# A hybrid attention and convolution layer on one core: dependent work moved between the steps of a slot

## The chip, the cores and the metric

The kernel runs on one NeuronCore of a Trainium2 chip. The metric is the device time of one execution in microseconds (us). The engines are TensorE (PE in the profile, its weight loads PEld), VectorE (DVE), ScalarE (ACT), GpSimd (POOL), and SyncE (SP), whose queue issues the loads. They run side by side, each in its own order, and wait for each other through semaphores.

## What is computed

One layer on 272 tokens (16 learned ones and 256 given ones) of width 4096, in fp32, batch 1, cut from the reference:

```python
h = rmsnorm(x, norm_g)
p = h @ w_in                       # 4096 -> 16384
q, k, v, g_attn, b_conv, c_conv, h_conv, z_conv = split(p)     # 2048 each
# 16 heads x 128, strictly causal stick-breaking attention
z = q k^T / sqrt(128)
after = reverse_cumsum(log_keep) - log_keep       # log_keep = log_sigmoid(-z), masked
o = where(mask, exp(log_sigmoid(z) + after), 0) @ v
o = group_rmsnorm(o * silu(g_attn), attn_norm_g, 16)
y = b_conv * short_conv(c_conv * h_conv, conv_w)  # depthwise, causal, 3 taps
y = group_rmsnorm(y * silu(z_conv), conv_norm_g, 16)
out = rmsnorm(x + concat([o, y]) @ w_out, final_norm_g)[16:]
```

## The kernel before

**Split products.** An fp32 product is made of three fp32r products, high by high, low by high and high by low. Each piece of weights (128 rows by 1024) arrives by DMA as `raw`; ScalarE casts it to the high part `wh` (line 411), VectorE subtracts to get the low part `wl` (`low`, line 407). Rings of six `wh` and six `wl` stand between these two engines and TensorE. The loop at line 1018 goes through `pieces`: at piece i it issues TensorE's work of i, ScalarE's cast of piece i+4, then the tasks that are due at i (`run_tasks`), then VectorE's low part of piece i+4 (`lows`). A task thus stands behind a cast and ahead of a low in the queues. The order is fixed by hand.

**Groups and slots.** The 32 heads and convolution channels are worked as eight groups of two units. For a group, q, the attention gate, b and z are made with tokens on partitions, two row blocks at a time, by a seven-product scheme (Strassen-like) over 15 of the 16 pairs of weight pieces; k, v, c and h are made per unit with features on partitions ("blocks": `mm`, four pieces of 24 matmuls each, 272 or 258 wide). The list interleaves both. A **slot** is one pair in the seven-product form and half a block: the pieces A, B, T, U, then two pieces p; T and U have no load, as their weights are sums that VectorE makes from A's and B's (lines 428, 431, 433, so B has four VectorE instructions: t, raw, wl, raw). Slots are numbered 0 to 14; slot 12 has no block. TensorE has 6, 3, 6, 6, 24 and 24 matmuls in the six pieces, those of A, B, T, U 512 wide. In a slot's six steps the fourth is U and the fifth the first p. The cast that ScalarE issues at U is that of the next slot's B, at the first p that of the next T, at the second p that of the next U.

**Zones.** Zone S of group g are its 15 slots, with blocks k, v, c, h of the first unit and k, v, c of the second; they end with slots 1, 3, 5, 7, 9, 11 and 14. The finished block is evicted by VectorE (kT, vt, cc) in the tasks of the next piece. Then comes zone R: the h block of the second unit in four pieces, with one plain pair (A, B, 12 matmuls each) of the next group in the middle. There the seven products of the group are evicted to `cq` (q and gate) and `cb` (b and z) by `evict`, eight VectorE operations of line 661.

**Banks.** PSUM has eight banks. In zone S seven hold products, and one, `d + D22`, is shared by the blocks and by all small outputs (po, ct, mx): `spare(i)` gives this list of one. In zone R three banks are spare, in the order of D22, D12, D21 of the group that has just ended; `bank` takes them in turn by a counter that runs through the whole kernel.

**The dependent work of a group** is done in the next group's zones R and S, by generators whose `yield k` puts what follows k pieces later: `silu`, `q_t` (q transposed on TensorE, copied back by ScalarE), `scores` (z, then tanh and ln on ScalarE), `weights` per head (Relu on ScalarE, two scans and a subtraction on VectorE, four Exp on ScalarE), `trans` (a 32x32 transpose on VectorE, then small ScalarE copies into `at`, in four blocks of four, and two more), `po` (the product with v, then VectorE's gate), `conv_t` and `conv_out` (the convolution transposed on TensorE, copied by ScalarE, gated on GpSimd), `squares` and `norm`, and `mix` (transposes on TensorE, ScalarE's scaling, and a DMA to `mixd` from ScalarE's queue). `v_block` and `h_block` plan v's transpose and copies (`vv`, four blocks and `v3`) and the three taps (`conv`: one ScalarE and two VectorE operations). Before the change, for group g in the slots c of group g+1 (`t[c]` is B of slot c):

```python
later(t[1], weights, g, 0)    # t[3] for the second head
later(t[2], trans, g, 0)      # after(t[4], 1) for the second
later(t[4], po, g, 0)         # t[6]
later(t[7], squares, g, "h")  # "c" two pieces after t[9]
later(t[8], conv_t, ...)      # conv_out two pieces later
later(t[10], norm, g)
later(t[12], mix, g, "h")     # "c" two pieces later
```

Tiles that are used by turns bound the order too: `zm`, `zs` and `u2` hold the stages of the attention and also vt, yv, silu's factor and mixing's outputs.

After group 7 follows the output projection, by the same seven-product scheme and with split pieces, and the final normalisation; `at`, the transposes and the norm of group 7 run at its beginning.

Of the kernel before, what the change touches and what calls it, by code (L numbers as in the profile page):

```python
# [15 lines left out]
P = 128  # L16
# [106 lines left out]
def kernel(ctx, tc, xt, xin, xm, par, fg, w1, w2, out):  # L123
# [15 lines left out]
    def bank(nm, i=None):  # L139

        if i is None:
            i = free[0][turn[0] % len(free[0])]
            turn[0] += 1
        return pp.tile([P, 512], F32, tag=f"b{i}", name=nm)
# [385 lines left out]
    def later(at, fn, *args):  # L530
        tasks.append((at, fn, args))
# [53 lines left out]
        V.tensor_tensor(out=kt, in0=src, in1=rstd, op=ALU.mult)  # L585
        hd[u, "k"] = kt

    def v_block(u, src, at_):
        vt = wk.tile([P, 448], F32, tag="zm", name=f"vt{u}")
        G.memset(vt[:, L:L + META], 0.0)  # L590
        V.tensor_tensor(out=vt[:, :L], in0=src, in1=rstd, op=ALU.mult)

        def vtrans():
            y = wk.tile([P, 416], F32, tag="zs", name=f"yv{u}")
            V.transpose(out=y[:, :L + META], in_=vt[:, :L + META])
            yield 1
            vv = wk.tile([P, 2 * P], F32, tag=f"vv{u % 2}", name=f"vv{u}")
            for i in range(4):
                blocks(vv, y[:, :2 * P], 2, i, (A.copy,))
                yield 1  # L600
            v3 = wk.tile([META, P], F32, tag=f"v3{u % 2}", name=f"v3{u}")
            for i in range(4):
                A.copy(out=v3[:, 32 * i:32 * i + 32], in_=y[32 * i:32 * i + META, 2 * P:2 * P + 32])
            hd[u, "v"] = (vv, v3)

        later(at_, vtrans)
# [6 lines left out]
    def h_block(u, src, at_):  # L613
        c = hd.pop((u, "c"))
        V.tensor_tensor(out=c, in0=src, in1=c, op=ALU.mult)  # L615

        def conv():
            y = wk.tile([P, SEQ], F32, tag=f"cy{u % 2}", name=f"cy{u}")
            w = [pt[:, CW0 + 3 * u + i:CW0 + 3 * u + i + 1] for i in range(3)]
            A.mul(out=y, in_=c[:, 0:SEQ], mul=w[0])  # L620
            yield 1
            V.scalar_tensor_tensor(out=y, in0=c[:, 1:SEQ + 1], scalar=w[1], in1=y, op0=ALU.mult, op1=ALU.add)
            V.scalar_tensor_tensor(out=y, in0=c[:, 2:SEQ + 2], scalar=w[2], in1=y, op0=ALU.mult, op1=ALU.add)
            cy[u] = y

        later(at_, conv)

    def plain_block(u, b, e):
        ps = psum.pop((u, b, "p"))
        if b == 0:  # L630
            k_block(u, ps[:, :L])
        elif b == 1:
            v_block(u, ps[:, :L], after(e, 1 if u < 2 else 6 if u % 2 else 13))
        elif b == 2:
            c_block(u, ps[:, META - 2:L])
        else:
            h_block(u, ps[:, META - 2:L], after(e, (12 if u else 8) if u % 2 == 0 else 8 if u < 15 else 1))


    gr = {}  # L640
# [44 lines left out]
    def squares(g, q):  # L685

        y = gr[g][q][1]
        if "ss" not in gr[g]:
            gr[g]["ss"] = wk.tile([P, 8], F32, tag="sm3", name=f"ss{g}")
        ss = gr[g]["ss"]  # L690
        j = wk.tile([P, P], F32, tag="junk", name=f"j{q}{g}")
        f = 0 if q == "h" else 4
        for t in range(2):
            for u in range(2):
                c = f + 2 * u + t
                A.activation(out=j, in_=y[:, t, u], func=AF.Square, scale=(rt if q == "h" else rt2)[:, t:t + 1],
                             accum_out=ss[:, c:c + 1])

    def norm(g):

        ss = gr[g]["ss"]
        r = rsqrt_raw(ss, P, EPS, *small(f"n{g}_"))
        V.tensor_tensor(out=ss, in0=r, in1=fac, op=ALU.mult)
        for f, q in ((0, "h"), (4, "c")):
            yield 1
            y = gr[g][q][1]
            for t in range(2):
                for u in range(2):
                    c = f + 2 * u + t
                    A.mul(out=y[:, t, u], in_=y[:, t, u], mul=ss[:, c:c + 1])  # L710
# [22 lines left out]

    def q_t(g):
        q = gr[g]["h"][0]
        o = bank(f"qT{g}")
        for u in range(2):
            for t in range(2):
                c = (2 * u + t) * P
                T.transpose(out=o[:, c:c + P], in_=q[:, t, u], identity=ident)  # L740
        yield 1
        A.copy(out=q, in_=o.rearrange("p (u t x) -> p t u x", u=2, t=2))

    def scores(g):
        q = gr[g]["h"][0]
        z, zm, l = {}, {}, {}
        for u in range(2):
            kt = hd[2 * g + u, "k"]
            z[u] = bank(f"z{g}_{u}")
            T.matmul(out=z[u][:, :144], lhsT=q[:, 0, u], rhs=kt[:, :144], start=True, stop=True)  # L750
            T.matmul(out=z[u][:, 144:ZW], lhsT=q[:, 1, u], rhs=kt, start=True, stop=True)
        yield 1
        for u in range(2):
            zm[u] = (wk.tile([P, 512], F32, tag="u2", name=f"zm{g}_{u}", bufs=2) if u else
                     wk.tile([P, 448], F32, tag="zm", name=f"zm{g}_{u}"))[:, :ZW]
            l[u] = wk.tile([P, 448], F32, tag=f"zl{u}", name=f"zl{g}_{u}")[:, :ZW]
            V.scalar_tensor_tensor(out=zm[u][:, :144], in0=z[u][:, :144], scalar=rq[:, 0:1], in1=zmask[:, P:],
                                   op0=ALU.mult, op1=ALU.add)
            V.scalar_tensor_tensor(out=zm[u][:, 144:], in0=z[u][:, 144:ZW], scalar=rq[:, 1:2], in1=zmask,
                                   op0=ALU.mult, op1=ALU.add)  # L760
            A.activation(out=l[u], in_=zm[u], func=AF.Abs)
        for u in range(2):
            A.activation(out=l[u], in_=l[u], func=AF.Tanh, scale=0.5)
        yield 1
        for u in range(2):
            A.activation(out=l[u], in_=l[u], func=AF.Ln, scale=0.5, bias=half)
            gr[g]["z", u] = zm[u], l[u]

    def weights(g, u):
        zm, l = gr[g].pop(("z", u))  # L770
        s = wk.tile([P, 416], F32, tag="zs", name=f"zs{g}_{u}")
        A.activation(out=s, in_=zm, func=AF.Relu)
        yield 1
        for c, n in ((0, 144), (144, L)):
            V.tensor_tensor_scan(out=l[:, c:c + n][:, ::-1], data0=s[:, c:c + n][:, ::-1],  # L775
                                 data1=l[:, c:c + n][:, ::-1], initial=0.0, op0=ALU.add, op1=ALU.subtract)
        V.tensor_tensor(out=s, in0=zm, in1=l, op=ALU.subtract)
        yield 1

        za = wk.tile([P, 512], F32, tag="u2", name=f"za{g}_{u}", bufs=2) if u else wk.tile([P, 448], F32, tag="zm", name=f"za{g}_{u}")  # L780
        za = za[:, :448]
# [8 lines left out]
    def trans(g, u):  # L790
        za = gr[g].pop(("za", u))
        y = wk.tile([P, 448], F32, tag=f"zl{u}", name=f"ya{g}_{u}")
        V.transpose(out=y, in_=za)
        yield 1
        for i in range(4):
            blocks(at[:, P:], y[:, :3 * P], 3, i, (A.copy,) if g < GROUPS - 1 else (A.copy, V.tensor_copy))
            if i < 3 and (g < GROUPS - 1 or i == 1):
                yield 1
        A.copy(out=at[:META, P - META:P], in_=y[96:96 + META, 400:416])
        A.copy(out=a3[:, P - META:], in_=y[96:96 + META, 432:448])  # L800

# [33 lines left out]

    def after(i, k):

        return real[min(nth[i] + k, len(real) - 1)]

    def slot(g, c):  # L840

        return pieces.index(("B", g, sevens(g)[c]))

    def plan_group(g):
        f = fin[g]
        e = ends[2 * g + 1, 3]
        end = g == GROUPS - 1
        later(after(f, 1), silu, g, "h")
        later(after(f, 2), q_t, g)
        later(after(f, 2), silu, g, "c")  # L850
        later(after(f, 4), scores, g)
        if not end:
            t = [slot(g + 1, c) for c in range(len(SJ))]
        later(after(f, 7) if end else t[1], weights, g, 0)
        later(after(f, 10) if end else t[3], weights, g, 1)
        later(after(f, 10) if end else t[2], trans, g, 0)
        if end:
            later(after(e, 5), conv_t, (2 * g, 2 * g + 1))
            later(after(e, 7), conv_out, g)
            later(after(f, 13), po, g, 0)  # L860
            later(after(f, 13), trans, g, 1)
            later(after(f, 17), po, g, 1)
            later(after(f, 17), squares, g, "c")
            later(after(f, 19), squares, g, "h")
            later(after(f, 20), norm, g)
            later(after(f, 22), mix, g, "h")
            later(after(f, 23), mix, g, "c")
            return
        later(t[4], po, g, 0)
        later(after(t[4], 1), trans, g, 1)  # L870
        later(t[6], po, g, 1)
        later(t[7], squares, g, "h")
        later(t[8], conv_t, (2 * g, 2 * g + 1))
        later(after(t[8], 2), conv_out, g)
        later(after(t[9], 2), squares, g, "c")
        later(t[10], norm, g)
        later(t[12], mix, g, "h")
        later(after(t[12], 2), mix, g, "c")


    res, fgs, acc, sqs = [], {}, [], []
# [274 lines left out]
```

## Time and profile before

| what | value |
|---|---|
| median of 3 runs (lowest to highest) | 1798.13 us (1797.33 to 1800.46) |
| the profiled execution, its own time | 1798.58 us |
| its span | 1796.9 us |
| granted TensorE clock over the span | 0.997 |
| HBM read and written | 391.70 MB, 13.11 MB |

In a line of the profile's groups stand the line of the kernel, the engine, the operation, what is written and read (buffer numbers left out) and its shape, the count, the busy time, the mean of one in ns, and the idle time of the engine just before with what ended it. A row of the view of waits has the engine and line that waited, what released it, the total in us, how often, and the longest. A timeline row has the start, the duration, engine, line, operation, tiles and shape; several alike are merged (x2). A row of the windows view has the stretch, its length, then for each engine its busy time and in brackets its instructions (PE, PEld, DVE, ACT, POOL), the granted clock, the DMA's busy share and GB/s. The chain that ended last runs for 89% of the span over TensorE and for 6% over VectorE. Group 5's dependent work lies in the slots of the next group, whose slot 1 begins at 1100.5 us.

### The profile page before, as it was taken

What the parts mean: (1) busy time and instruction counts of PE and PEld (TensorE: products, weight loads), DVE (VectorE), ACT (ScalarE), POOL (GpSimd) and SP (SyncE); (2) the same over time, 40 slices, a digit from 0 to 9 for tenths busy, and PEclk for the clock granted to TensorE, in tenths of its full rate; (3) what the DMA queues carried; (4) which work ended last, traced back from release to release, by engine and by line L of the source; (5) the groups of instructions that cost most, each with busy time, mean ns of one, the idle gap of its engine ahead of it and who ended that gap; (6) DMA issues with size and microseconds to landing.
All of it is one profiled execution on the core that took longest, in us unless ns stands there. A gap on an engine that the chain in (4) does not pass through costs nothing.

```text
span 1796.9 us, 29780 instructions
## 1 busy us (share of the span) xinstructions
PE 1773.2 (99%) x10947; PEld 1604.8 (89%) x10947; DVE 1563.3 (87%) x1899; ACT 1225.1 (68%) x2081; POOL 148.3 (8%) x180
## 2 busy tenths in 40 slices
PE   9999999999999999999999999999999999999997
PEld 7899989998999899989898989899989988888897
DVE  6866888998899889988898889889988988889896
ACT  6754776767676767676767677767776786555553
POOL 2133101010101010001010101011001110000000
PEclk9999999999999999999999999999999999999999
DMA  8967666766666667666666666666666676676565
GB/s 314 322 231 247 203 219 225 230 214 222 224 224 213 224 223 225 216 223 224 222 212 223 223 224 210 223 223 226 208 225 222 223 250 233 223 237 219 196 216 196
DMA packets 119667, 406.77 MB, mean 226 GB/s; under 512 B 13408, under 2 KB 18656, under 8 KB 119520
## 3 DMA queue, kind: packets, MB, share of 16 engines
q1 hardware_dynamic: 115488, 401.19, 66.5%
q10 hardware_dynamic: 4032, 3.67, 0.6%
q8 instruction: 86, 1.41, 0.3%
q14 instruction: 61, 0.50, 0.1%
HBM read 391.70 MB, written 13.11 MB: 225 GB/s over the span
## 4 chain that ended last, share of the span: by engine, by line
PE 89%; DVE 6%; issue 2%; ACT 2%; DMA 1%; ACTq 0%; DVEq 0%; SPq 0%
PE P L452 17%; PE P L454 16%; PE P L455 16%; PE mm L445 12%; PE mm L444 12%; PE mm L446 12%; DVE wl L407 3%; ACT wh L411 1%; DVE t L428 1%; DVE cb L661 1%; PE mo L944 0%; PE mo L943 0%; PE mo L942 0%; PE po L808 0%; DVE zl L775 0%
## 5 line engine op out<-in xcount | busy, mean ns | idle before, releaser
L407 DVE TENSOR_TENSOR wl<-raw,wh 128x1024 fp32r<-128x1024 f32 (+3 forms) x773 | 867.5, 1146 | 142.1 <-ACT wh L411 130.0
L411 ACT CAST wh<-raw 128x1024 fp32r<-128x1024 f32 (+3 forms) x773 | 718.9, 967 | 237.3 <-DVE raw L433 78.7
L444 PE MATMUL mm<-xs,wh 128*128 128x258 f32 (+1 forms) x2048 | 583.4, 285 | 0.0
L446 PE MATMUL mm<-xs,wl 128*128 128x258 f32 (+1 forms) x2048 | 581.9, 284 | 1.0 <-DVE wl L407 1.0
L445 PE MATMUL mm<-xs,wh 128*128 128x258 f32 (+1 forms) x2048 | 581.7, 284 | 0.0
L444 PEld LDWEIGHTS mm<-xs,wh 128*128 128x128 f32 x2048 | 385.5, 188 | 4.3 <-ACT mfc L727 0.2
L445 PEld LDWEIGHTS mm<-xs,wh 128*128 128x128 f32 x2048 | 385.6, 188 | 4.1
L446 PEld LDWEIGHTS mm<-xs,wl 128*128 128x128 f32 x2048 | 385.6, 188 | 1.5 <-DVE wl L407 1.4
L411 ACT CAST wh<-t 128x1024 fp32r<-128x1024 f32 (+1 forms) x125 | 130.3, 1043 | 194.7 <-DVE t L428 171.2
L452 PE MATMUL P<-wh,xs 128*128 128x512 f32 x499 | 196.5, 394 | 2.6 <-ACT wh L411 1.9
L455 PE MATMUL P<-wl,xs 128*128 128x512 f32 x499 | 194.9, 391 | 0.0
L454 PE MATMUL P<-wh,xs 128*128 128x512 f32 x499 | 194.8, 390 | 0.0
L452 PE MATMUL P<-wh,mixl 128*128 128x512 f32 (+1 forms) x412 | 155.7, 378 | 0.0
L455 PE MATMUL P<-wl,mixh 128*128 128x512 f32 (+1 forms) x412 | 155.1, 377 | 0.0
L454 PE MATMUL P<-wh,mixh 128*128 128x512 f32 (+1 forms) x412 | 155.0, 376 | 0.0
L428 DVE TENSOR_TENSOR t<-raw,raw 128x1024 f32<-128x1024 f32 (+1 forms) x125 | 153.0, 1224 | 0.0
L407 DVE TENSOR_TENSOR wl<-t,wh 128x1024 fp32r<-128x1024 f32 (+1 forms) x125 | 152.5, 1220 | 0.0
L452 PEld LDWEIGHTS P<-wh,xs 128*128 128x128 f32 x499 | 94.0, 188 | 24.5 <-DVE cc L615 3.0
L455 PEld LDWEIGHTS P<-wl,xs 128*128 128x128 f32 x499 | 94.1, 189 | 20.0
L454 PEld LDWEIGHTS P<-wh,xs 128*128 128x128 f32 x499 | 94.1, 189 | 19.4
L452 PE MATMUL P<-wh,lent 128*128 128x512 f32 x280 | 111.3, 397 | 0.0
L455 PE MATMUL P<-wl,lent 128*128 128x512 f32 x280 | 109.3, 390 | 0.0
(240 smaller groups left out, 2128.8 us busy)
## 6 DMA issues: line engine op xcount, KB each, us to landing
raw<-w SPq DMA_DIRECT2D x614, 512.0 KB, 4.3
lent<-sumd SPq DMA_DIRECT2D x70, 512.0 KB, 5.6
raw<-w SPq DMA_DIRECT2D x32, 384.0 KB, 3.9
sumd<-lent SPq DMA_DIRECT2D x10, 512.0 KB, 4.7
raw<-xin SPq DMA_DIRECT2D x8, 512.0 KB, 5.1
raw<-mixd SPq DMA_DIRECT2D x8, 512.0 KB, 4.5
xr<-xt SPq DMA_DIRECT2D x15, 272.0 KB, 5.0
res<-xin SPq DMA_DIRECT2D x12, 256.0 KB, 4.7
```

What stands on the lines that cost most here:

```text
L407: nc.vector.tensor_tensor(out=lo[:, c], in0=t[:, c], in1=h[:, c].bitcast(F32), op=ALU.subtract)
L411: nc.scalar.copy(out=h[:, c], in_=t[:, c])
L428: nc.vector.tensor_tensor(out=s[:, :2 * hw].rearrange("p (a b) -> p a b", a=2), in0=a[:, :2 * hw].rearrange("p (a b) -> p a b", a=2), in1= ...
L444: nc.tensor.matmul(out=o, lhsT=h, rhs=x[:, 0, s:], start=k == 0, stop=False)
L445: nc.tensor.matmul(out=o, lhsT=h, rhs=x[:, 1, s:], start=False, stop=False)
L446: nc.tensor.matmul(out=o, lhsT=lo, rhs=x[:, 0, s:], start=False, stop=k == KC - 1)
L452: nc.tensor.matmul(out=o, lhsT=a[1], rhs=h, start=key not in begun, stop=False)
L454: nc.tensor.matmul(out=o, lhsT=a[0], rhs=h, start=False, stop=False)
L455: nc.tensor.matmul(out=o, lhsT=a[0], rhs=lo, start=False, stop=last)
L661: V.tensor_tensor(out=o, in0=x, in1=y, op=op)
```

## The change

The dependent work is put at other pieces. `slot(g, c, q)` now gives the piece of kind q (A, B, T, U, "p" or "q" for the second p) of a slot, and a generator may `yield "U"` or `yield "p"`: what follows goes to the next U, or to the next first p of a slot (outside zone S to the next piece). In group g+1's slots the work of group g now stands so: head 0's Relu at U of 2, its scans at p of 2, its Exp at U of 3; head 1's at p of 3, p of 4, p of 5. The transposes of the weights at p of 3 and T of 6, their copies two blocks at the next U, one at the p, one and the small ones at the U after. The convolution's transposes go from slot 8 to B of 4, `conv_out` to U of 4, po to B of 6 and B of 8, squares of c to p of 7 and U of 8, those of h to U of 9, the norm to A of 10 with all its eight muls at U of 10; mixing stays at B and U of 12. v's VectorE transpose goes to p of 8 and U of 12, its copies to p of 9 and following, and, for the second unit, to U and p of slots 0 and 1 of the next group; the taps' first operation to U of 8, or U of slot 1, and VectorE's part to the p after. q takes the third spare bank of zone R (D21), the scores' two the second and the first. The last group keeps its places except for what `yield` joins and splits.

```diff
-    def v_block(u, src, at_):
+    def v_block(u, src, at_, at2):
...
-            yield 1
+            later(at2, vcopies, y)
+
+        def vcopies(y):
             vv = wk.tile([P, 2 * P], F32, tag=f"vv{u % 2}", name=f"vv{u}")
-            for i in range(4):
+            for i, k in enumerate((0, 1, 1, 1) if u < 2 else (0, 0, "p", "U") if u % 2 else (0, "p", "U", 0)):
+                if k:
+                    yield k
                 blocks(vv, y[:, :2 * P], 2, i, (A.copy,))
-                yield 1
+            yield 1 if u < 2 else "p"
...
             A.mul(out=y, in_=c[:, 0:SEQ], mul=w[0])
-            yield 1
+            yield "p"
...
-            v_block(u, ps[:, :L], after(e, 1 if u < 2 else 6 if u % 2 else 13))
+            g = u // 2
+            v_block(u, ps[:, :L], *((after(e, 1), after(e, 2)) if not g else
+                                    (slot(g, 12, "U"), slot(g + 1, 0, "U") if u < 15 else slot(g, 13, "U")) if u % 2 else
+                                    (slot(g, 8, "p"), slot(g, 9, "p"))))
...
-            h_block(u, ps[:, META - 2:L], after(e, (12 if u else 8) if u % 2 == 0 else 8 if u < 15 else 1))
+            h_block(u, ps[:, META - 2:L], slot(u // 2 + 1, 1, "U") if u % 2 and u < 15 else
+                    slot(u // 2, 8, "U") if u % 2 == 0 and u else after(e, 1 if u else 8))
...
         for t in range(2):
+            if t and q == "c":
+                yield "U"
...
         for f, q in ((0, "h"), (4, "c")):
-            yield 1
+            if q == "h":
+                yield "U"
...
-        o = bank(f"qT{g}")
+        o = bank(f"qT{g}", free[0][2])
...
-            z[u] = bank(f"z{g}_{u}")
+            z[u] = bank(f"z{g}_{u}", free[0][1 - u])
...
         A.activation(out=s, in_=zm, func=AF.Relu)
-        yield 1
+        yield "p"
...
         V.tensor_tensor(out=s, in0=zm, in1=l, op=ALU.subtract)
-        yield 1
+        yield "p" if u else "U"
...
         V.transpose(out=y, in_=za)
-        yield 1
+        last = g == GROUPS - 1
         for i in range(4):
-            blocks(at[:, P:], y[:, :3 * P], 3, i, (A.copy,) if g < GROUPS - 1 else (A.copy, V.tensor_copy))
-            if i < 3 and (g < GROUPS - 1 or i == 1):
-                yield 1
+            if i != 1 and not (last and i == 3):
+                yield 1 if last else "UUpU"[i]
+            blocks(at[:, P:], y[:, :3 * P], 3, i, (A.copy, V.tensor_copy) if last else (A.copy,))
...
     def after(i, k):
 
+        if k in ("U", "p"):
+            return next((j for j in range(i + 1, min(i + 12, n1)) if pieces[j][0] == k and (k == "U" or pieces[j][2] % 2 == 0)),
+                        after(i, 1))
         return real[min(nth[i] + k, len(real) - 1)]
 
-    def slot(g, c):
-
-        return pieces.index(("B", g, sevens(g)[c]))
+    def slot(g, c, q="B"):
+
+        i = pieces.index(("A", g, sevens(g)[c]))
+        return i + "ABTUpq".index(q)
...
+            at_ = lambda c, q: slot(g + 1, c, q)
+            later(at_(2, "U"), weights, g, 0)
+            later(at_(3, "p"), weights, g, 1)
+            later(at_(3, "p"), trans, g, 0)
+            later(at_(4, "B"), conv_t, (2 * g, 2 * g + 1))
+            later(at_(4, "U"), conv_out, g)
+            later(at_(6, "B"), po, g, 0)
+            later(at_(6, "T"), trans, g, 1)
+            later(at_(7, "p"), squares, g, "c")
+            later(at_(8, "B"), po, g, 1)
+            later(at_(9, "U"), squares, g, "h")
+            later(at_(10, "A"), norm, g)
+            later(at_(12, "B"), mix, g, "h")
+            later(at_(12, "U"), mix, g, "c")
```

More of the change, by code (lines that the diff above doesn't have):

```diff
@@ L852, in plan_group @@
         if not end:
[L853 to L867, printed above, removed]
-            return
@@ L869, in plan_group @@
[L869 to L878, printed above, removed]
+            at_ = lambda c, q: slot(g + 1, c, q)
+            later(at_(2, "U"), weights, g, 0)
+            later(at_(3, "p"), weights, g, 1)
@@ new lines, in plan_group @@
+            return
+        later(after(f, 7), weights, g, 0)
+        later(after(f, 10), weights, g, 1)
+        later(after(f, 10), trans, g, 0)
+        later(after(e, 5), conv_t, (2 * g, 2 * g + 1))
+        later(after(e, 7), conv_out, g)
+        later(after(f, 13), po, g, 0)
+        later(after(f, 13), trans, g, 1)
+        later(after(f, 17), po, g, 1)
+        later(after(f, 17), squares, g, "c")
+        later(after(f, 19), squares, g, "h")
+        later(after(f, 20), norm, g)
+        later(after(f, 22), mix, g, "h")
@@ L881 @@
+        later(after(f, 23), mix, g, "c")
     res, fgs, acc, sqs = [], {}, [], []
```

## The prediction

> **What bounds the kernel now.** I read the page first: its busy times, then two long stretches of the windows view.
>
> ```profile
> PE 1773.2 (99%) x10947; PEld 1604.8 (89%) x10947; DVE 1563.3 (87%) x1899; ACT 1225.1 (68%) x2081; POOL 148.3 (8%) x180
> ```
>
> ```profile
> 20.00:1750.00 1730.00, 1720.49 (x10615) 1554.94 (x10614) 1522.68 (x1816) 1196.58 (x2038) 143.81 (x168) 1.00 0.68 227
> 1750.00:1797.00 47.00, 35.68 (x265) 35.48 (x264) 28.31 (x61) 16.39 (x27) 0.00 (x0) 0.92 0.53 194
> ```
>
> TensorE is the bound. Between 20 and 1750 us it is busy 1720.49 of 1730.00: 9.5 us idle. The last 47 us hold 11.3 us more, but that is the closing chain, which the diff leaves alone. The change keeps every matmul and every transpose, so it can only shift waits. Next, TensorE's own waits, then one from its weight-load side:
>
> ```profile
> PE po L804 <- DVE vt L591: 6.5, 7, 1.1
> ...
> PE mm L446 <- DVE wl L407: 1.0, 2, 0.6
> PE P L452 <- DVE cc L615: 0.6, 2, 0.3
> ...
> PE qT L740 <- DVE cc L610: 0.6, 2, 0.3
> ```
>
> ```profile
> PEld mxc L716 <- issue: 2.9, 7, 0.4
> ```
>
> Seven waits of some 0.9 us, one for each of groups 0 to 6, precede the first attention output (po). Six smaller ones lie where a group ends. The seven of mxc happen where the mixing transposes wait for their bank, which the change keeps. A waiting matmul costs slightly more than its idle time, as the timeline of TensorE shows at the po of group 5:
>
> ```profile
> 1132.32 0.29 PE L445 MATMUL mm<-xs,wh 128*128 128x272 f32 x1
> 1132.44 0.28 PE L446 MATMUL mm<-xs,wl 128*128 128x272 f32 x1
> ...
> 1134.15 0.39 PE L454 MATMUL P<-wh,xs 128*128 128x512 f32 x1
> 1134.38 0.39 PE L455 MATMUL P<-wl,xs 128*128 128x512 f32 x1
> 1135.89 0.49 PE L804 MATMUL po<-vv,at 128*128 128x128 f32 x2 [1.12 <-DVE vt L591]
> ```
>
> 512-wide matmuls start 0.23 us apart though each lasts 0.39 (the 272-wide ones 0.12 apart), so the 1.51 us before po holds a loss of 1.28, not 1.12: add 0.16 to each wait. The thirteen waits then cost 8.7 + 13 x 0.16 = **10.8 us**. That is what the change can win; the ceiling with everything else idle in the stretch is about 9.5 + 20 x 0.16 = 12.7.
>
> The Trainium skill, "Perfetto Trace Analysis", section "Identifying the Most-Contended Engine", says that matmul occupancy misjudges the distance from the roofline and that LDWEIGHTS occupancy should be used. By that, 89% would leave 192 us; the start-to-start spacing above shows no such room, since a 512-wide matmul holds the array 0.23 us whatever its weight load takes.
>
> **Why po waits.** po's bank is the one that the finished block (v) leaves, and VectorE must have evicted it (vt). VectorE's timeline:
>
> ```profile
> 1122.24 1.23 DVE L407 TENSOR_TENSOR wl<-raw,wh 128x1024 fp32r<-128x1024 f32 x1 [0.23 <-ACT wh L411]
> 1124.76 2.36 DVE L407 TENSOR_TENSOR wl<-raw,wh 128x1024 fp32r<-128x1024 f32 x2 [1.30 <-ACT wh L411]
> 1127.04 1.07 DVE L775 TENSOR_TENSOR_SCAN zl<-zs,zl 128x144 f32<-128x144 f32 x2
> ...
> 1128.65 1.22 DVE L407 TENSOR_TENSOR wl<-raw,wh 128x1024 fp32r<-128x1024 f32 x1
> 1129.79 1.22 DVE L428 TENSOR_TENSOR t<-raw,raw 128x1024 f32<-128x1024 f32 x1
> 1131.04 0.69 DVE L431 TENSOR_TENSOR raw<-raw,t 128x512 f32<-128x512 f32 x1
> 1131.65 0.69 DVE L407 TENSOR_TENSOR wl<-raw,wh 128x512 fp32r<-128x512 f32 x1
> 1132.37 0.69 DVE L433 TENSOR_TENSOR raw<-raw 128x512 f32<-128x512 f32 x1
> 1132.98 1.22 DVE L407 TENSOR_TENSOR wl<-t,wh 128x1024 fp32r<-128x1024 f32 x1
> 1134.26 1.23 DVE L407 TENSOR_TENSOR wl<-raw,wh 128x1024 fp32r<-128x1024 f32 x1
> 1135.40 0.43 DVE L591 TENSOR_TENSOR vt<-mm,rstd 128x272 f32<-128x272 f32 x1
> ```
>
> The block ended near 1132.7, po could have begun at 1134.61, the eviction ended at 1135.83. VectorE had lost 0.23 + 1.30 = 1.53 us to ScalarE and spent 1.61 (1127.04 to 1128.65) on the second head's scans. ScalarE in the same slot:
>
> ```profile
> 1120.01 1.11 ACT L578 COPY at<-ya 32x96 f32<-32x96 f32 x4
> 1121.15 1.06 ACT L411 CAST wh<-raw 128x1024 fp32r<-128x1024 f32 x1
> 1122.23 1.11 ACT L578 COPY at<-ya 32x96 f32<-32x96 f32 x4
> ...
> 1123.68 2.00 ACT L411 CAST wh<-raw 128x1024 fp32r<-128x1024 f32 x2
> ```
>
> Four copies of 0.28 us stand ahead of each cast, so the cast at 1123.68, for which VectorE waits, is late. And yet ScalarE sits idle every slot for VectorE:
>
> ```profile
> ACT wh L411 <- DVE t L428: 171.2, 95, 4.3
> ...
> ACT wh L411 <- DVE raw L433: 78.7, 74, 1.8
> ```
>
> These are 1.8 us at the fifth piece (its cast is that of the next T, which needs t) and 1.06 at the sixth (the next U, which needs raw). Work issued at U falls into the first hole, work at the first p into the second.
>
> **The change, part by part.** A slot is A B T U p p. On TensorE it lasts 21 x 0.227 + 48 x 0.12 = 10.6 us; on VectorE 4.47 for the B and T pieces (1129.79 to 1134.26) and four lows at 1.18, 9.2: spare 1.4 a slot.
>
> - First slots. Relu, scans and exponentials of head 0 go from slot 1 to 2, those of head 1 from slot 3 to 3-5. The 1.61 us of scans leave the way of vt, and the copies of `at` go to U and p: the 1.53 us goes too. Together 3.1 us, more than the 1.22 by which vt was late; it would then be bound by the block's end, 1132.7, and leave the bank at 1133.2. The convolution's transposes, which take po's place at B of slot 4 and wait for the same eviction, would have 1.4 us to spare. Were they late, T and U of slot 4 would stand behind them on TensorE, and on ScalarE the cast of the next B behind the copies of cy.
> - Slots 4 and 5. Head 1's scans (1.66) now stand here, and so does conv_out on GpSimd, which moves from slot 8. It costs VectorE time; the trace has it at slot 9, VectorE with conv_out beside it:
>
> ```profile
> 1003.69 1.48 DVE L428 TENSOR_TENSOR t<-raw,raw 128x1024 f32<-128x1024 f32 x1
> 1005.21 0.84 DVE L431 TENSOR_TENSOR raw<-raw,t 128x512 f32<-128x512 f32 x1
> 1005.97 1.23 DVE L407 TENSOR_TENSOR wl<-raw,wh 128x512 fp32r<-128x512 f32 x1
> 1007.23 0.84 DVE L433 TENSOR_TENSOR raw<-raw 128x512 f32<-128x512 f32 x1
> 1007.99 1.48 DVE L407 TENSOR_TENSOR wl<-t,wh 128x1024 fp32r<-128x1024 f32 x1
> ```
>
> ```profile
> L683 POOL TENSOR_TENSOR cb<-cb,cy 128x128 f32<-128x128 f32 x32 | 33.9, 1080 | 462.6 <-ACT cy L821 461.9
> ...
> L680 POOL TENSOR_TENSOR cb<-cb 128x256 f32<-128x256 f32 x16 | 21.3, 1333 | 0.0
> ```
>
>  The five take 5.87 instead of 4.51: 1.36 us lost beside 4 x 1.08 + 2 x 1.33 = 7.0 us of GpSimd. From 1133.2 VectorE needs 2 x 9.2 + 1.66 + 1.36, then 0.43 to evict (c): 1155.1. po, now at B of slot 6, could begin 2.0 us after a block end at 1132.7 + 21.2 + 0.4: 1156.3. 1.2 us remain, so I cost this at nothing; if that cover goes, each further us is paid seven times.
> - Bursts at U. Eight copies (2.2 us) exceed the 1.8 us hole by 0.4; v's two blocks are eight shorter copies; the norm's eight muls (row below, 3.1 us at most) exceed it by 1.3, but in slot 10, where the next bank is due only at slot 12. Between 0 and 1.3 us of VectorE delay each; I take 0, as the spare covers it.
>
> ```profile
> L710 ACT ACTIVATE cq<-cq,ss 128x128 f32<-128x128 f32 x32 | 10.3, 392 | 15.6 <-DVE ss L703 15.6
> ```
>
> - Group's end. v's copies of the odd head went between the last casts; they move behind the eviction, to U of slot 0. In group 4 they and a late chain make VectorE wait:
>
> ```profile
> 884.13 1.23 DVE L407 TENSOR_TENSOR wl<-raw,wh 128x1024 fp32r<-128x1024 f32 x1 [0.87 <-ACT wh L411]
> 886.00 3.50 DVE L407 TENSOR_TENSOR wl<-raw,wh 128x1024 fp32r<-128x1024 f32 x3 [0.65 <-ACT wh L411]
> ```
>
>  These 1.52 us precede the eviction of the rows and everything after it up to h's (cc). With ScalarE free there, the two waits for wl (1.3 us with the 0.16) and those for cc L615 (0.9) should end. Fixed banks give q the bank that the rows' eviction frees, never that of the last (c) block: the two qT waits (0.9) end.
> - Squares, norm, mixing: the same instructions in other slots, with mixing where it was; the DMAs of mixd are issued by ScalarE where they were, no load passes another on SP's queue, and GpSimd's conv_out is queued ahead of a memset (za) that is needed slots later. The last group only splits and joins pieces: 0.
>
> Sum: -10.8; I keep 0.8 for waits that don't quite close: **-10.0**. The profiled run took 1798.58 with a span of 1796.9; the median is 1798.13, 1.2 above that span. 1786.9 + 1.2 = **1788.1**.
>
> **The rivals.**
>
> 1. Only po's waits go: 6.5 + 7 x 0.16 = 7.6, less 0.6. The waits at the end of a group come from the DMA of mixd as well, which stays. 1798.1 - 7 = 1791. For it: they differ from group to group. Chance 0.18.
> 2. The wait changes its name: conv_t at slot 4 waits for vt as po did, or VectorE is 1 us late at po in slot 6. Only the 3 us elsewhere are won: 1795. Against it: 3.1 us leave vt's way; for it: 1.2 us of spare is little. Chance 0.17.
> 3. Slower: GpSimd's operations hold VectorE for their whole length. It then loses 7.0 instead of 1.36 us in slots 4 and 5; 5.6 more, less the spare of 1.2, is 4.4 us before po in each of seven groups, 31 in all: 1819. It turns the sign from some 4.5 us lost (1.36 + 1.2 + (10.0 + 3.6) / 7). The five rows above speak against it; for it, the scans were never seen beside GpSimd. Chance 0.07.
>
> The Trainium skill has this as a rule: "SBUF — State Buffer", section "Who interferes with whom", says that a VectorE operation with two SBUF inputs contends with a GpSimd one that reads SBUF, and the summary that the second to issue blocks until the first is done. Those rows show a stretch of 1.2 to 1.8 times, no standstill.
>
> **How the numbers follow.** Forecast 0.58, of 1786 to 1790. Same within 0.2% (3.6 us, about what a measurement of this kernel can tell) is rival 2: 0.17; slower is rival 3: 0.07; faster 0.76. The range goes from all 12.7 us won, 1785, to rival 2 with a us on top, 1796, and leaves out rival 3 and little else.
>
> **What would show it.** The waits of TensorE: no po <- vt and no ct <- vt in its place; po at slots 6 and 8 without idle time; VectorE's waits for wh gone in slot 3; qT without cc L610; mxc as before. Po or ct with an eviction as releaser would prove rival 2; VectorE operations over 2 us at conv_out rival 3. Wrong from the root would be a span above 1797 with these waits gone: then TensorE's own spacing, or the loads, would have changed.

## The result and the profile after

| | before | after |
|---|---|---|
| median of 6 runs each | 1798.36 us | 1786.2 us |
| span of the profiled execution | 1796.9 us | 1784.2 us |
| TensorE busy, idle in the span | 1773.2, 23.7 us | 1769.1, 15.1 us |

The changed kernel takes 0.9931 of the time before (95% interval 0.9917 to 0.9945): 12.2 us less by the medians, where 10.0 were forecast. One of its six runs took 2187.38 us at a granted clock of 0.751; the ratio leaves it out, and the median moves by 0.1 us with it.

The page after, busy times, and the long middle stretch in the windows view (its length, then the busy time of PE, PEld, DVE, ACT, POOL):

```profile
PE 1769.1 (99%) x10947; PEld 1604.4 (90%) x10947; DVE 1563.1 (88%) x1899; ACT 1228.1 (69%) x2081; POOL 149.7 (8%) x180
```

```profile
20.00:1739.00 1719.00, 1718.16 (x10623) 1556.69 (x10622) 1523.67 (x1817) 1199.74 (x2038) 145.34 (x168) 1.00 0.67 228
```

Of the 9.5 us that TensorE was idle in the middle, 0.84 are left. VectorE and ScalarE do the same work as before to a few us. TensorE's waits, all of them, and from its weight-load side the one that the change was to keep:

```profile
PE P L452 <- ACT wh L411: 1.5, 1, 1.5
PE warm L151 <- DVE ones L148: 1.1, 1, 1.1
PE P L455 <- DVE wl L407: 1.0, 3, 0.6
```

```profile
PEld mxc L727 <- issue: 3.0, 7, 0.5
```

Those of the first two rows and two of the last row lie in the opening; the third of that row, 0.61 us at 1490.80 in the output projection, stood in the kernel before as well. No wait of po, of the convolution's transposes (ct), of q's transposes or of a block for an eviction stands there any more. VectorE's timeline in slots 3 to 6 of the same group 5:

```profile
1119.65 0.64 DVE L804 STREAM_TRANSPOSE ya<-za 128x448 f32<-128x448 f32 x1
1120.21 1.18 DVE L407 TENSOR_TENSOR wl<-t,wh 128x1024 fp32r<-128x1024 f32 x1
1121.32 1.77 DVE L407 TENSOR_TENSOR wl<-raw,wh 128x1024 fp32r<-128x1024 f32 x1
1123.58 0.44 DVE L591 TENSOR_TENSOR vt<-mm,rstd 128x272 f32<-128x272 f32 x1 [0.50 <-PE mm L446]
...
1128.86 0.84 DVE L431 TENSOR_TENSOR raw<-raw,t 128x512 f32<-128x512 f32 x1
1129.62 1.23 DVE L407 TENSOR_TENSOR wl<-raw,wh 128x512 fp32r<-128x512 f32 x1
...
1131.64 1.33 DVE L786 TENSOR_TENSOR_SCAN zl<-zs,zl 128x144 f32<-128x144 f32 x2
...
1145.02 0.43 DVE L614 TENSOR_TENSOR cc<-mm,rstd 128x258 f32<-128x258 f32 x1
```

VectorE now waits 0.50 us for the block before it evicts vt: it is early where it was 1.22 us late. The scans (1131.64) come after the operations that conv_out stretches (1.23 where 0.69 is usual), and the eviction of (c) for po ends at 1145.45. TensorE reaches po then:

```profile
1146.65 0.39 PE L455 MATMUL P<-wl,xs 128*128 128x512 f32 x1
1146.88 0.38 PE L815 MATMUL po<-vv,at 128*128 128x128 f32 x2
1147.10 0.39 PE L816 MATMUL po<-vv,at 128*128 128x128 f32 x2
```

The spacing of 0.23 us runs on into po. The next line of po starts 0.22 us after the first. In the kernel before, where po at 1135.89 had waited, it took 0.32:

```profile
1136.21 0.39 PE L805 MATMUL po<-vv,at 128*128 128x128 f32 x2
```

A matmul that had to wait thus also costs the one behind it 0.1 us; it is 0.32 or 0.33 at all seven waits of po in the kernel before.

### The profile page after: what moved, and what is told of

It reads as the page before. It is cut to its first block, busy times and chain, and to the rows that moved or that the text cites. A ratio compares the mean times of both kernels' runs of the same rounds, so it can differ in the third digit from the quotient of the medians.

```text
span 1784.2 us, 29778 instructions
## 1 busy us (share of the span) xinstructions
PE 1769.1 (99%) x10947; PEld 1604.4 (90%) x10947; DVE 1563.1 (88%) x1899; ACT 1228.1 (69%) x2081; POOL 149.7 (8%) x180
## 4 chain that ended last, share of the span: by engine, by line
PE 98%; DVE 1%; DMA 0%; ACT 0%; SPq 0%; POOL 0%; issue 0%; DVEq 0%
PE P L452 18%; PE P L455 17%; PE P L454 17%; PE mm L444 14%; PE mm L445 14%; PE mm L446 14%; PE mo L961 0%; PE mo L960 0%; PE mo L959 0%; PE z L762 0%; PE po L819 0%; DMA raw<-w 0%; PE mxc L727 0%; PE z L761 0%; PE po L816 0%; PE po L818 0%
## 5 line engine op out<-in xcount | busy, mean ns | idle before, releaser
L407 DVE TENSOR_TENSOR wl<-raw,wh 128x1024 fp32r<-128x1024 f32 (+3 forms) x773 | 864.0, 1147 | 95.0 <-ACT wh L411 87.4
L452 PE MATMUL P<-wh,xs 128*128 128x512 f32 x499 | 195.7, 392 | 1.5 <-ACT wh L411 1.5
L452 PE MATMUL P<-wh,mixl 128*128 128x512 f32 (+1 forms) x412 | 155.7, 378 | 0.0
L452 PEld LDWEIGHTS P<-wh,xs 128*128 128x128 f32 x499 | 93.7, 188 | 22.9 <-ACT wh L411 1.8
L452 PE MATMUL P<-wh,lent 128*128 128x512 f32 x280 | 111.4, 398 | 0.0
```

Source lines behind the costliest of these rows:

```text
L407: nc.vector.tensor_tensor(out=lo[:, c], in0=t[:, c], in1=h[:, c].bitcast(F32), op=ALU.subtract)
L452: nc.tensor.matmul(out=o, lhsT=a[1], rhs=h, start=key not in begun, stop=False)
```

## The experiments

The theory: two delays of VectorE, either of which may stay, made vt late, and each group's end had smaller waits of its own. The main rivals: the order alone (convolution ahead of attention), the banks, or ScalarE's places within a slot. Each run is compared with the kernel before on its own chip; 0.001 is 1.8 us, and the intervals are 0.001 to 0.0014 to either side. The changed kernel stands at 0.9931.

### The banks alone

```diff
 # the kernel before
-        o = bank(f"qT{g}")
+        o = bank(f"qT{g}", free[0][2])
-            z[u] = bank(f"z{g}_{u}")
+            z[u] = bank(f"z{g}_{u}", free[0][1 - u])
```

> The kernel before with the fixed banks for q and the scores alone. Theory (each wait costs for itself): the two waits of q's transposes for the eviction of cc end, 2 x (0.3 + 0.16) = 0.9 us less than before, and nothing else moves: 1797.4. Rival (banks unimportant, a late eviction is the cause): q's transposes wait in another group or for another eviction, within 0.3 us of before.

0.9994 (0.9985 to 1.0004). The time can't tell 0.9 us from nothing. The waits can: q's transposes no longer wait, and po's stay.

```profile
PE po L804 <- DVE vt L591: 7.0, 7, 1.1
```

### The banks taken back

```diff
 # the changed kernel
-        o = bank(f"qT{g}", free[0][2])
+        o = bank(f"qT{g}")
-            z[u] = bank(f"z{g}_{u}", free[0][1 - u])
+            z[u] = bank(f"z{g}_{u}")
```

> The changed kernel with the banks of q and the scores taken in turn again. Theory (a bank freed by the last block's eviction is late by itself): two waits of q's transposes for cc come back, 0.9 us more than the changed kernel, 1787.1. Rival (with the evictions in time the bank doesn't matter): 0, 1786.2.

0.9928 (0.9916 to 0.9941), as the changed kernel, and no wait of q's transposes in the profile: the rival holds. With the evictions in time it doesn't matter which of the three banks q takes.

### The order alone, twice

```diff
 # the kernel before
-        later(t[4], po, g, 0)
-        later(after(t[4], 1), trans, g, 1)
-        later(t[6], po, g, 1)
-        later(t[7], squares, g, "h")
-        later(t[8], conv_t, (2 * g, 2 * g + 1))
-        later(after(t[8], 2), conv_out, g)
-        later(after(t[9], 2), squares, g, "c")
+        later(t[4], conv_t, (2 * g, 2 * g + 1))
+        later(after(t[4], 2), conv_out, g)
+        later(t[6], po, g, 0)
+        later(after(t[6], 1), trans, g, 1)
+        later(t[7], squares, g, "c")
+        later(t[8], po, g, 1)
+        later(after(t[9], 2), squares, g, "h")
...
-            v_block(u, ps[:, :L], after(e, 1 if u < 2 else 6 if u % 2 else 13))
+            v_block(u, ps[:, :L], after(e, 1 if u < 2 else 6 if u % 2 else 15))   # second run: 25
```

> The kernel before with the order alone: the convolution's transposes at B of slot 4, po at B of 6 and of 8, squares of c first; scans, copies and banks where they were (v's even copies two pieces later, as po reads that tile at slot 6). Theory (the eviction of vt is late, whoever waits): the wait passes to ct, seven times some 0.9 us idle, 1798 as before within 1. Rival (po was the wrong thing to have at slot 4, the order is what wins): waits for vt gone, 7 us less, 1791.

1.0290 (1.0276 to 1.0304), 53 us slower. The waits of TensorE:

```profile
PE po L804 <- DVE cc L615: 20.7, 7, 3.0
PE ct L818 <- DVE vt L591: 6.6, 7, 1.1
```

The theory's part came as expected: ct waits for vt as po did. The 20.7 us nobody had expected. In this run v's copies and those of the second head's weights fell on the same pieces, and VectorE waited for one cast after another:

```profile
1204.44 1.23 DVE L407 TENSOR_TENSOR wl<-raw,wh 128x1024 fp32r<-128x1024 f32 x1 [1.24 <-ACT wh L411]
1207.66 1.23 DVE L407 TENSOR_TENSOR wl<-raw,wh 128x1024 fp32r<-128x1024 f32 x1 [2.00 <-PE P L454]
1211.10 1.23 DVE L407 TENSOR_TENSOR wl<-raw,wh 128x1024 fp32r<-128x1024 f32 x1 [2.21 <-ACT wh L411]
1215.40 1.22 DVE L407 TENSOR_TENSOR wl<-raw,wh 128x1024 fp32r<-128x1024 f32 x1 [3.08 <-ACT wh L411]
```

The second run moves v's copies out of the way.

> As the order alone, but with v's even copies four slots later than before (from A of slot 8), so that no piece has two blocks of copies. Theory: the waits of ct for vt stay (7 x 0.9 idle), the 20.7 us of po at slot 8 and the half clock after them go, since they came from eight copies a piece: 1796 to 1800. Rival (po at slots 6 and 8 is itself too early in this order): po still waits for cc, over 1805.

1.0023 (1.0015 to 1.0032), 4 us slower. Its median of 1802.55 lies 2.5 us above the theory's range and 2.5 below the rival's 1805: the theory's wait came, and so did a small one of the rival's.

```profile
PE ct L818 <- DVE vt L591: 6.5, 7, 1.1
PE po L804 <- DVE cc L615: 2.6, 7, 0.6
```

Ct takes over po's 6.5 us, po waits 2.6 on top. Those 2.6 us with 7 x 0.26 (0.16 of start spacing and 0.1 of the matmul behind for each wait) are 4.4. The order by itself wins nothing.

### The scans ahead of vt again

```diff
 # the changed kernel
-            later(at_(2, "U"), weights, g, 0)
-            later(at_(3, "p"), weights, g, 1)
+            later(at_(2, "B"), weights, g, 0)
+            later(at_(3, "B"), weights, g, 1)
...
-        yield "p"                      # after Relu
+        yield 1
...
-        yield "p" if u else "U"        # after the scans
+        yield 1
```

> The changed kernel with both heads' Relu, scans and Exp at B, T, U of slots 2 and 3, so that head 1's scans (1.66 us) stand ahead of vt again; copies, order and banks as changed. Theory (two delays made vt late, either may stay): vt's eviction has 2.0 us to spare in the changed kernel (it waits 0.5 for the block's end, and ct could wait 1.5 more), so 1.66 cost nothing: 1786 to 1787, no wait of ct. Rival (the scans alone made the wait): ct waits for vt, seven times about 0.5 to 1 us, 1790 to 1793.

0.9933 (0.9920 to 0.9945), and no wait of ct: the scans alone don't make ct wait. In group 5 the eviction of vt ends at 1125.63 and ct starts at 1125.89; 0.26 us are left.

### The copies ahead of slot 3's casts again

```diff
 # the changed kernel
-            later(at_(2, "U"), weights, g, 0)
+            later(at_(2, "B"), weights, g, 0)
-            later(at_(3, "p"), trans, g, 0)
+            later(at_(2, "p"), trans, g, 0)
...
-        yield "p"                      # after Relu
+        yield "p" if u else 1
...
-        yield "p" if u else "U"        # after the scans
+        yield "p" if u else 1
...
-            if i != 1 and not (last and i == 3):
-                yield 1 if last else "UUpU"[i]
+            if not last and not u or i != 1 and not (last and i == 3):
+                yield 1 if last or not u else "UUpU"[i]
```

> The changed kernel with head 0's weights at B, T, U of slot 2, its transposition at the first p of slot 2 and one block of copies at each piece after it, which puts them ahead of casts in slot 3 as before; head 1's scans stay at slot 4. Theory: VectorE waits some 1.5 us for casts in slot 3 again, which the 2.0 us to spare cover: 1786 to 1787. Rival (ScalarE's copies alone made the wait): ct waits for vt, 7 x 0.5 or more, 1790 to 1793.

0.9948 (0.9936 to 0.9960), some 3 us more than the changed kernel: between the two, and a miss of the theory's amount. The two intervals overlap, but on the same chip the five runs lie above all five of the run before (1788.32 to 1791.37 against 1786.07 to 1787.12), and ct waits:

```profile
PE ct L829 <- DVE vt L591: 1.5, 7, 0.2
```

```profile
1116.86 2.91 DVE L407 TENSOR_TENSOR wl<-raw,wh 128x1024 fp32r<-128x1024 f32 x2
1120.76 1.23 DVE L407 TENSOR_TENSOR wl<-raw,wh 128x1024 fp32r<-128x1024 f32 x1 [0.99 <-ACT wh L411]
1122.97 1.23 DVE L407 TENSOR_TENSOR wl<-raw,wh 128x1024 fp32r<-128x1024 f32 x1 [0.98 <-ACT wh L411]
...
1129.72 0.43 DVE L591 TENSOR_TENSOR vt<-mm,rstd 128x272 f32<-128x272 f32 x1
```

VectorE loses 0.99 + 0.98, some 2.0 us and not 1.5, to casts that stand behind copies. (The first row is no loss to them: one of its two lows takes 1.76 us beside a GpSimd operation, as the low at 1121.32 of the changed kernel with its 1.77.) And the spare is not quite 2.0. In the changed kernel ct starts here,

```profile
1125.42 0.60 PE L829 MATMUL ct<-ident,cy 128*128 128x128 f32 x4
```

1.40 us after vt's eviction ends (1123.58 + 0.44); with the 0.50 that VectorE waits, 1.9. Seven waits of 0.2, each with 0.16 and 0.1, make 3.3 us.

### Both

The scans' and the copies' edits together (Relu, scans and Exp by `yield 1` for both heads).

> The changed kernel with both of the two edits: scans of head 1 ahead of vt and copies ahead of the casts of slot 3. Theory: 1.66 + 1.5 - 2.0 = 1.2 us late, ct waits for vt in seven groups, 7 x (1.2 + 0.1) = 9 us more, 1795. Rival (the order or the later place of po is what won): 1786 to 1788.

0.9969 (0.9958 to 0.9981), 7 us more than the changed kernel:

```profile
PE ct L829 <- DVE vt L591: 5.3, 7, 0.8
```

5.3 + 7 x 0.26 = 7.1. It is the wait of before under another name. The two delays overlap in part, so 9 was too much:

```profile
1121.49 1.23 DVE L407 TENSOR_TENSOR wl<-raw,wh 128x1024 fp32r<-128x1024 f32 x1 [0.99 <-ACT wh L411]
1122.63 1.06 DVE L786 TENSOR_TENSOR_SCAN zl<-zs,zl 128x144 f32<-128x144 f32 x2
...
1124.24 1.22 DVE L407 TENSOR_TENSOR wl<-raw,wh 128x1024 fp32r<-128x1024 f32 x1
```

The scans run while the second cast is late, so VectorE waits for one cast only: 0.99 + 1.61 (1122.63 to 1124.24) is 2.6, 0.7 more than the 1.9 to spare.

### ScalarE's copies at any piece

```diff
 # the changed kernel
-            if i != 1 and not (last and i == 3):
-                yield 1 if last else "UUpU"[i]
+            if not last or i != 1 and i != 3:
+                yield 1
```

> The changed kernel with the four blocks of copies of both heads one at each piece from the piece after the transposition on, not at U and p; nothing else moves. Theory (the places U and p matter): VectorE waits for casts in slots 4 and 6 to 7 again, some 2 us a head; po at slot 6 is up to 1 us late: 1787 to 1794. Rival (only what lies ahead of vt matters): 1786 to 1787, with VectorE's waits for wh no longer than in the changed kernel.

0.9931 (0.9917 to 0.9944), the time of the changed kernel: the rival's time. VectorE does wait more for casts,

```profile
DVE wl L407 <- ACT wh L411: 100.4, 114, 4.9
```

against 87.4 us in 104 waits in the changed kernel, but in slots that had the time to spare. For these copies the fourth and fifth step of a slot are no better than others; what counts is that they no longer hold up a cast that VectorE needs before vt's eviction, which still waits 0.50 us for the block here.

### v's copies before the end of a group again

```diff
 # the changed kernel
-                                    (slot(g, 12, "U"), slot(g + 1, 0, "U") if u < 15 else slot(g, 13, "U")) if u % 2 else
+                                    (slot(g, 13, "B"), slot(g, 13, "T")) if u % 2 else
...
-            for i, k in enumerate((0, 1, 1, 1) if u < 2 else (0, 0, "p", "U") if u % 2 else (0, "p", "U", 0)):
+            for i, k in enumerate((0, 1, 1, 1) if u < 2 or u % 2 else (0, "p", "U", 0)):
...
-            yield 1 if u < 2 else "p"
+            yield 1 if u < 2 or u % 2 else "p"
```

> The changed kernel with the odd head's v copies back between the last casts of a group (one block a piece from T of slot 13), the rest as changed. Theory: VectorE waits for casts again before the rows are evicted, and the waits of TensorE for wl and cc come back in some groups: 1 to 3 us more, 1787 to 1789. Rival (the chain over the DMA of mixd made those waits, and the copies only lay beside it): 0, 1786.2.

0.9943 (0.9930 to 0.9955), 2 us more; 3.5 between the medians of different chips, and 2.7 above the run with the banks taken back, on the same chip. The intervals overlap, so the time alone doesn't show it; the edit also moves v's transposition on VectorE, from U of slot 12 to B of 13. But TensorE waits again at the ends of groups, as in the kernel before:

```profile
PE P L452 <- DVE cc L619: 1.3, 4, 0.3
...
PE mm L446 <- DVE wl L407: 0.2, 1, 0.2
```

### How much VectorE has to spare

```diff
 # the changed kernel
         V.tensor_tensor(out=s, in0=zm, in1=l, op=ALU.subtract)
+        for _ in range(2 * u):                                    # second run: 5 * u
+            V.tensor_tensor(out=zm, in0=zm, in1=l, op=ALU.subtract)
```

> The changed kernel with head 1's subtraction at the first p of slot 4 followed by two more of its kind, whose result nobody reads: some 2 x 0.55 = 1.1 us of VectorE ahead of the eviction that po at slot 6 waits for. Theory: that eviction has 1.5 us to spare (it ends at 1145.45 in group 5, po starts at 1147.0): 0 more, 1786.2. Rival (the spare is used up, the evictions are just in time): 7 x 1.1 = 8 us more.

0.9939 (0.9926 to 0.9951), 1.4 us above the changed kernel: near the theory's 0. The profile has one new wait, 0.8 us at po of the last group, whose second head has the two operations as well; po at slot 6 does not wait: in group 5 the eviction of (c) ends at 1146.72, po starts at 1147.13. With the 0.26 of a wait, the new one makes 1.1 of the 1.4 us.

> The same with five: 2.75 us of VectorE. Theory: 2.75 - 1.5 = 1.25 late, with the 0.26 of a restart, seven times: 10 us more, 1796, and po at slot 6 waits for cc. Rival (VectorE makes it up before slot 6): 0.

1.0022 (1.0013 to 1.0030), 16 us above the changed kernel instead of 10.

```profile
PE P L455 <- DVE wl L407: 7.0, 8, 0.9
PE po L817 <- DVE at L578: 2.6, 1, 2.6
PE po L817 <- DVE cc L614: 1.6, 7, 0.2
```

```profile
1142.56 3.10 DVE L790 TENSOR_TENSOR zm<-zm,zl 128x416 f32<-128x416 f32 x5
```

The five take 3.10 us, not 2.75. TensorE first lacks the low parts (some 0.9 a group), then (c)'s eviction (0.2), and the last group loses 2.6 once. A group's two waits cost 0.9 + 0.2 + 2 x 0.26 = 1.6 us, so of the 3.10 some 1.5 were to spare, as expected, though the low parts run out before the eviction does. Seven groups at 1.6 and the last one's 2.6 make 14 of the 16 us; the rest is within the two intervals.

### A version that beats both

```diff
 # the changed kernel
-            later(at_(12, "U"), mix, g, "c")
+            later(at_(13, "A"), mix, g, "c")
```

> The changed kernel with the convolution's mixing transposes one piece later, at A of slot 13 and not U of 12, so that ScalarE has emptied their bank. Theory: the seven waits of mxc (start to start 0.2 us each above the spacing) end and no block waits for the bank: 1.4 us less, 1784.8. Rival: the next block, at the first p of slot 13, waits for the mixing's eviction instead, or ScalarE's later work makes the rows' eviction late: 1786 to 1788.

0.9923 (0.9910 to 0.9937), median 1784.78, the lowest of all. The seven waits of mxc are gone. What is new is small:

```profile
PE mm L444 <- ACT mfc L738: 0.2, 1, 0.2
```

The 1.4 us between its median and that of the changed kernel is as expected, but the two intervals overlap. On its own chip its five runs (1784.48 to 1784.88) all lie below those of the run with the scans ahead of vt (1786.07 to 1787.12), whose TensorE waits as the changed kernel's does, with the mxc row; that and the row that vanished are the evidence.

## Why the prediction was right

**The bound and what can be won.** Right: TensorE's idle time in the middle went from 9.5 to 0.84 us, and the thirteen waits with their 8.7 us went. The term mis-sized is the price of a wait, "add 0.16 to each wait": it leaves out the 0.1 us by which the matmul behind a waiting one is late. With 0.26, 8.7 + 13 x 0.26 is 12.1, against 12.2 measured (the 0.1 is read at the seven waits of po, and the two of mm and the two of P L452 show the same; for q's two it is taken). The 0.8 us "that don't quite close" was needless caution: all closed.

**Why vt was late.** Both delays named are real. But "the 1.53 us goes too", because copies fall into holes at U and p, took the wrong reason: the copies at any piece give the same time. What freed slot 3 is that the copies no longer hold up casts that VectorE needs before vt's eviction. The scans by themselves (0.9933) make no wait, the copies by themselves (0.9948) one of 0.2 us a group, both together (0.9969) one of 0.75.

**Slots 4 and 5.** Right: 1.2 us were computed to remain, 1.4 are there by the timeline (1145.45 to 1146.88) and 1.5 by the dose of five operations. (By its own terms the slot is 10.53 us rather than 10.6, which makes the computed spare 1.1.) GpSimd stretches VectorE as the five rows of the kernel before say. Rival 3 did not come: no operation of VectorE that runs beside conv_out lasts 2 us, and the longest beside any GpSimd operation of this stretch takes 1.77. It was hardly put to the test with the scans: their first 0.4 us run beside the end of conv_out's last operation (1130.38 to 1132.04), and the two take 1.33 us where 1.07 is usual.

**Group's end.** Right: the odd head's v copies are worth some 2 us, by the waits for wl and cc. Rival 1, that the DMA of mixd alone makes those waits, falls, since the DMA's place is as before.

**The banks.** "The two qT waits end" is right, but for a reason not needed: they end without the fixed banks too. In the changed kernel these lines cost and win nothing that can be seen.

**Rival 2** is what the order alone does: ct took over the wait for vt to the tenth of a us (6.5 of 6.5). It didn't come about only because scans and copies moved with it.

By the runs, of the 12.2 us some 7 go to scans and copies in slot 3, 2 to 3.5 to v's copies. The rest, some 2 to 3 us, was not separated; the two waits of q's transposes (0.6 + 2 x 0.26 = 1.1) may be part of it.

## What to carry to other kernels

When one engine is busy 99% and another feeds it a few pieces ahead, count for each shared bank how late its eviction may be, and list what stands in the feeder's queue ahead of it; a wait needs the sum of several delays, and removing any that brings the sum under the spare is enough. Changing only who uses the bank hands the wait on. Where inside a slot an engine with spare time does its work matters less than which deadline it lies ahead of; but work of two kinds on the same pieces can starve the feeder for several pieces in a row.

## What the runs showed of the hardware

A wait can cost far more than its length. In the first run of the order alone TensorE was idle 2.95 us before po, and the windows view shows its granted clock (the column after the five engines) afterwards:

```profile
1222.40:1226.00 3.60, 3.40 (x12) 2.86 (x13) 2.98 (x5) 1.91 (x3) 0.00 (x0) 0.50 0.71 196
1226.00:1230.00 4.00, 4.00 (x13) 3.14 (x12) 3.93 (x5) 1.05 (x1) 0.00 (x0) 0.62 0.54 218
1230.00:1234.00 4.00, 4.00 (x35) 4.00 (x34) 2.54 (x3) 2.08 (x2) 0.00 (x0) 1.00 0.46 146
```

The clock is at half for some 7 us, and back at full by 1230. The same view shows 0.50 for the first 6 us after this wait in all seven groups, and 0.76 to 0.97 for the 6 us behind them; by these figures the lower clock costs 27 us. TensorE's waits after the opening are 35.0 us, 26 more than the 9.3 of the kernel before. Together that is the 53. The wait of 2.65 us in the last group with five extra operations has no such drop behind it (a granted clock of 1.00 in the 11 us after it), nor do those of 1.1 us before po in the kernel before (1.00 from 20 to 1750 us). One thing isn't separated: in each of the seven groups a wait of 0.7 to 0.8 us ends 0.5 us before the long one begins, so the two together may be what lowers the clock. The Trainium skill, "TensorE: Matmul & The Clock Gate", section "Why this matters for your kernels", puts the limit for idle gaps at about 3 us; the waits of 2.95 and 2.65 us agree with it.

The second finding is the 0.1 us that a matmul loses behind one that waited, 0.32 instead of 0.22 us at po, on top of the 0.16 us that the waiting one loses beyond the idle time shown.
